# A hybrid RWKV-7 / Mamba-2 / mixture-of-experts kernel: the recurrence pairs' operands through DRAM, and the chain as a stream of its own

## The chip, the cores and the metric

The kernel runs on one core of a Trainium2 chip. The metric is the device time in microseconds (us) of one execution. The profile is that of one execution, taken by the hardware profiler. Engines: PE (TensorE, matmul), PEld (its weight loads), DVE (VectorE), ACT (ScalarE), POOL (GpSimd) and SP (SyncE, which here issues nearly all DMAs).

## What is computed

Two layers over 256 context and 256 latent tokens of width 1024, float32. What matters here is the mixing block of each layer: an RWKV-7 branch (16 heads of 64, scanned in both directions), a Mamba-2 branch (32 heads in 8 groups), two gates, and then a mixture of 32 experts. The recurrence of the RWKV-7 branch, of one head and one direction:

```python
def wkv7_scan(r, w, k, v, a, b, s0, reverse, emit):
    def step(S, inp):
        r_t, w_t, k_t, v_t, a_t, b_t = inp
        sa = jnp.einsum("bhij,bhj->bhi", S, a_t)
        S = S * w_t[:, :, None, :] + sa[..., None] * b_t[:, :, None, :] + v_t[..., None] * k_t[:, :, None, :]
        y = jnp.einsum("bhij,bhj->bhi", S, r_t) if emit else None
        return S, y
    xs = tuple(jnp.moveaxis(t, 1, 0) for t in (r, w, k, v, a, b))
    S, ys = lax.scan(step, s0, xs, reverse=reverse)
    return S, (jnp.moveaxis(ys, 0, 1) if emit else None)
```

The context tokens come first in each scan, and their final state starts the scan of the latent tokens. In the second layer only the latent tokens are put out.

## The kernel before

**Stages.** Each layer has a head (modulation, norm), the mixing stage, a merge (branch projections `psbr`, output projection `pso`), routing, and the experts. In the mixing stage three kinds of work run beside each other: 8 RWKV pairs of two heads each (`rw_prep`, `rw_solve`, `rw_chain`, `rw_out`), 8 Mamba groups (`ssm_group`) and 8 gate blocks (`gates`); layer 0 also computes the modulation of later stages there.

**A pair.** The 512 tokens are cut into 8 chunks of 64. The two heads of a pair lie in the two halves of the 128 partitions.

- `rw_prep` (L1056) projects r, k, v, and transposes v into `SU`. For each direction d, `rw_dir` (L1152) makes the decayed operands: `X` and its transpose `XT`, `Z` (the a and r rows), and with matmuls `psg` the triangular matrices `QA` (within a chunk) and `AR` (for the output).
- `rw_solve` (L1238) inverts the triangular 64x64 systems of all chunks, heads and directions at once: 31 steps on DVE, each a multiplication into `slM` and a sum into `slY`, each needing the one before. `rw_merge` completes the inverses `TT` with PE.
- `rw_chain` (L1318) turns operands by `TT` (`psat`, `psav`, `psta`, `psua`; the copies go to `at`, `av`, `QA`, `SU`), makes the chunk transitions `GT` and the output terms, and then steps the state over the chunks: 7 steps, each a matmul `psH<-St,GT` on PE and a copy `St<-psH` on DVE (direction 0) and ACT (direction 1), each needing the one before. `psY` gathers the output.
- `rw_out` (L1406) normalizes, gates, and stores the result for the merge in DRAM (`rwd`).

**The order of the work.** Nothing is issued as it is written. A `Recorder` takes all calls of a layer down, and `schedule` (L519) orders them with a list scheduler: each engine in turn gets the call that can start first by the planner's costs, ties by the latest start that still meets the due time of its stream. A stream is a label with a due time, set by `rec.at` in `mix_streams` (L1672). A call that opens a tile must find a free place: `SLOTS` says how many tiles of a name may live at once, `CLASS` how many places there are of each size. The program that results is fixed: each engine runs its own calls in that order, and waits for others by semaphores.

**What a pair holds.** `SLOTS` allows two tiles each of `SU`, `Z`, `XT`, `AR`, `QA`, `TT`, one for each direction, so one pair at a time. `rw_dir` opens them, and before the change `rw_chain` is the last to read `SU`, `Z`, `XT`, `AR` and, as a place for the turned operands, `QA`. The next pair's `rw_dir` can open its own only when that chain has read them. All four parts of a pair form one stream, with one due time:

```python
        for i in range(8):
            rec.at(1, ("rw", i), h + 60e3 + P * (i + 1))
            self.rw_prep(l, i)
            self.rw_solve(i)
            rec.tight = True
            self.rw_chain(l, i)
            rec.tight = False
            self.rw_out(l, i)
```

All recorded calls carry the line of `emit` (L682 in the profile before, L683 after the change), so the rows are told apart by tile names.

Of the kernel before, what the change touches and what calls it, by code (L numbers as in the profile page):

```python
# [21 lines left out]
NT = 512  # L22
# [52 lines left out]
def _unit_rows():  # L75

    h = (np.arange(128) // 16) % 2
    s = 2 * np.arange(16)[None, :] + h[:, None]
    return (s[:, :, None] == np.arange(32)).astype(np.float32)
# [129 lines left out]
SLOTS = {"R": 2, "sp": 2, "t5": 4, "y5": 3, "rt5": 5, "ot": 2, "z1": 4, "wst": 2, "wh": 2, "wl": 2, "rwst": 1, "rwh": 1, "rwl": 1, "r": 1,  # L209
# [3 lines left out]
CLASS = {"c4": 18, "c2": 40, "c1": 23, "ps": 8}  # L213
# [8 lines left out]
ENGINES = tuple(LAT)  # L222

# [34 lines left out]
class _Pool:  # L258
# [3 lines left out]
    def tile(self, shape, dtype, name=None, tag=None, bufs=None):  # L262
        bufs = bufs or self.bufs
        tag = tag or name
        if not self.rec.on or self.real is None:
            return self.real.tile(shape, dtype, name=name, tag=tag, bufs=bufs)
        tag = ALIAS.get(tag, tag)
        ph = self.rec.phase
        if ph == 1:
            if self.psum and tag == "g":  # L270
                tag = "t"
            if tag in SPLIT and self.rec.stream[0] in ("rw", "sh"):
# [413 lines left out]
class Kernel:  # L686
# [10 lines left out]
    def setup(self):  # L697

        self.cp = self.pool("cp")
        self.dram = self.pool("dram", space=bass.MemoryType.DRAM)  # L700
        t = lambda n, s, d=F32: self.cp.tile(s, d, name=n)
        cst = self.cst = t("cst", [128, C_WA])
        self.c = lambda o, n=128: cst[:, o:o + n]
        self.ident = cst[:, C_ID:C_ID + 128]
        self.idb = t("idb", [128, 128], BF16)
        self.unit = t("unit", [128, 512], BF16)
        self.tri = t("tri", [128, 256], F16)
        self.io = t("io", [128, 256])
        self.iota, self.low = self.io[:, 0:128], self.io[:, 128:256]
# [12 lines left out]
        self.gd = self.dram.tile([128, 16, NT], F32, name="gd")  # L722
        self.ys = self.dram.tile([N_EXP * CAP[0], D], F32, name="ys")

    def constants(self):
# [4 lines left out]
        u = t([128, 512], F32, "unit32")  # L730
        nc.sync.dma_start(u, i["unit"].rearrange("p j t -> p (j t)"))
        nc.vector.tensor_copy(self.unit, u)
        nc.sync.dma_start(self.io, i["cst"][:, C_WS:C_T64F])
# [322 lines left out]
    def rw_prep(self, l, i):  # L1056
# [23 lines left out]
        vp = rp.tile([128, 64 + NT + 64], F32, name="v", bufs=2)  # L1080
        G.memset(vp[:, 0:64], 0.0)
        G.memset(vp[:, 64 + NT:], 0.0)
        v = S["v"] = vp[:, 64:64 + NT]
# [26 lines left out]
        for w0_ in (0, 4, 8):  # L1110
            pv = self.psum("t", [128, 4, 128], "psv")
            n = min(4, 9 - w0_)
            for w in range(n):
                T.transpose(pv[:, w], vp[:, 64 * (w0_ + w):64 * (w0_ + w) + 128], self.ident)
            if w0_ < 8:
                A.activation(SU[0][64:128, w0_:w0_ + 4, 0], pv[64:128, :, 0:64], AF.Copy)
            a = 0 if w0_ else 1
            A.activation(SU[0][0:64, w0_ + a - 1:w0_ + n - 1, 1], pv[0:64, a:n, 64:128], AF.Copy)
# [118 lines left out]

    def rw_solve(self, i):  # L1238
# [16 lines left out]
        G.tensor_copy(Y.rearrange("p j t -> p (j t)"), self.unit)  # L1255
# [62 lines left out]
    def rw_chain(self, l, i):  # L1318
# [14 lines left out]
        GT = wk.tile([128, 2, 8, 64], F32, name="GT", tag="slW")  # L1333
        St = wk.tile([128, 2, 8, 64], F32, name="St", tag="X")
        PH = []

        def batch(name, cs, out, lhs, rhs):

            ps = out or self.psum("g", [128, 8, 64], name)
            with nc.together():  # L1340
                for c in cs:
                    for e in E:
                        T.matmul(ps[rows[e], c], lhs(c, e), rhs(c, e), start=True, stop=True)
            return ps

        for d in range(2):
            SU = S["SU"][d]
            TT, XT, Z, AR = [S[x, d] for x in ("TT", "XT", "Z", "AR")]
            qa = S["QA", d].rearrange("p (c e) t -> p c e t", e=2)
            all8 = range(8)  # L1350
            mid = seq[d][1:7]

            ps = batch("psat", all8, None, lambda c, e: Z[rows[e], c, 0], lambda c, e: self.ident[rows[e], 64 * e:64 * e + 64])
            at = wk.tile([128, 8, 64], F32, name="at", tag="slY")
            A.activation(at, ps, AF.Copy)
            ps = batch("psav", all8, None, lambda c, e: qa[rows[1 - e], c, e], lambda c, e: SU[rows[1 - e], c, e])
            av = wk.tile([128, 8, 64], F32, name="av", tag="slB")
            V.tensor_copy(av, ps)
# [4 lines left out]
            ps = batch("psua", all8, None, lambda c, e: TT[rows[e], c], lambda c, e: av[rows[e], c])  # L1363
            A.activation(SU[rows[0], :, 0], ps[rows[0]], AF.Copy)
            V.tensor_copy(SU[rows[1], :, 1], ps[rows[1]])
            ps = batch("psgt", mid, None, lambda c, e: qa[rows[e], c, e], lambda c, e: XT[rows[e], c, 64 * e:64 * e + 64])
# [10 lines left out]
            ps = batch("psra", range(c0, 8), None, lambda c, e: qa[rows[e], c, e], lambda c, e: AR[rows[e], 2 * c + e])  # L1377
# [28 lines left out]
    def rw_out(self, l, i):  # L1406
# [12 lines left out]
        V.scalar_tensor_tensor(gw[64:96, 1], lo[64:96, 128:256], SW, gw[64:96, 1], op0=OP.mult, op1=OP.subtract)  # L1419
        y = wk.tile([128, NT], F32, tag="ot", name="gy", bufs=3)  # L1420
# [18 lines left out]
        G.tensor_tensor(y[:, :n], y[:, :n], S["bv"][:, :n], op=OP.add)  # L1439
# [232 lines left out]
    def mix_streams(self, l):  # L1672
# [50 lines left out]
    def route(self, l, X):  # L1723
# [63 lines left out]
        V.tensor_tensor(at, E1, E2, op=OP.add)  # L1787
        pp = self.psum("g", [128, nt, 32], "pspos")
        for t in range(nt):
            for u in range(t + 1):  # L1790
                T.matmul(pp[:, t], self.low if u == t else self.c(C_ONE), at[:, u], start=u == 0, stop=u == t)
# [391 lines left out]
```

## Time and profile before

| | us |
|---|---|
| median of 3 runs (3537.98 to 3549.52) | 3539.37 |
| the profiled execution, its own time | 3538.96 |
| its span | 3537.1 |
| PE busy | 3110.2 (88%) |
| PE weight loads busy | 2094.7 (59%) |
| DVE busy | 2447.3 (69%) |
| ACT busy | 1705.4 (48%) |
| POOL busy | 769.3 (22%) |

The span is the time from the first instruction to the last. "Busy" adds the times in which an engine executes; a busy PE is not a PE at its peak, since matmuls overlap. "Granted clock" is TensorE's clock as a share of full speed. The mixing stage of layer 0 lies at about 100 to 1185 us, its experts end at about 1930 us; the mixing stage of layer 1 lies at about 2000 to 2905 us, and its experts run to the end. A row with "idle ... <- X" tells how long an engine stood before such instructions, and what ended it.

### The profile page before, as it was taken

Reading aid. Unit: us, or ns where it says so; the run is one execution under the profiler, and the core shown is the slowest. Engines: PE = TensorE matmul, PEld = TensorE weight load, DVE = VectorE, ACT = ScalarE, POOL = GpSimd, SP = SyncE. Lnnn points to the kernel's source line nnn. Section 1 sums busy time; section 2 is a strip of 40 time slices with the busy share of each in tenths; the row PEclk is TensorE's granted clock in tenths of the full one; section 3 lists DMA queues with packets and bytes.
Section 4 is the critical chain, followed back from the end, with each engine's and each line's share of the span. In section 5 each row is a group of like instructions: output and inputs, shape, how many; then the busy total and the mean of one; then the engine's idle time right before and its main releaser. Section 6 shows DMA issues by size and latency. Waiting matters only on the chain. (4 is left out here: it accounts for less than half of the span.)

```text
span 3537.1 us, 86322 instructions
## 1 busy us (share of the span) xinstructions
PE 3110.2 (88%) x36050; PEld 2094.7 (59%) x36050; DVE 2447.3 (69%) x4491; ACT 1705.4 (48%) x3155; POOL 769.3 (22%) x1080
## 2 busy tenths in 40 slices
PE   7899889898998998999998778888889789899987
PEld 3566466475566457888886455666566668333332
DVE  4868868768778337999997788788988765221112
ACT  4554454454544325998886645554545434111111
POOL 1332332333232111111111133232333311000000
PEclk9999999999999997999999899999999889899998
DMA  7032231421312736999996411221212138999996
GB/s 283 28 106 73 93 118 51 151 100 43 120 57 98 276 104 222 412 401 397 396 394 249 154 63 45 74 69 50 75 61 71 53 125 299 346 399 398 399 398 243
DMA packets 241746, 662.65 MB, mean 187 GB/s; under 512 B 26688, under 2 KB 55104, under 8 KB 241344
## 3 DMA queue, kind: packets, MB, share of 16 engines
q1 hardware_dynamic: 236608, 640.22, 49.1%
q10 hardware_dynamic: 3584, 12.58, 0.9%
q8 instruction: 287, 4.70, 0.5%
q0 software_dynamic: 1152, 4.19, 0.3%
q14 instruction: 115, 0.94, 0.1%
HBM read 622.30 MB, written 34.60 MB: 186 GB/s over the span
## 5 line engine op out<-in xcount | busy, mean ns | idle before, releaser
L682 PE MATMUL mm<-h,wh 128*128 128x512 f16 (+1 forms) x2432 | 680.4, 363 | 11.0 <-ACT wh L682 11.0
L682 PEld LDWEIGHTS <-wh 128*128 128x128 f16 x3200 | 311.4, 99 | 280.7 <-issue 25.4
L682 PE MATMUL mm<-h,wl 128*128 128x512 f16 (+2 forms) x1216 | 439.0, 362 | 39.2 <-DVE wl L682 39.1
L682 DVE SCALAR_TENSOR_TENSOR ewl<-est,ewh 128x1024 f16<-128x1024 f32 x352 | 411.7, 1222 | 15.5 <-ACT ewh L682 12.4
L682 ACT ACTIVATE ewh<-est 128x1024 f16<-128x1024 f32 x384 | 382.6, 1049 | 32.4 <-PE pse L682 28.3
L682 DVE SCALAR_TENSOR_TENSOR wl<-wst,wh 128x1024 f16<-128x1024 f32 (+1 forms) x234 | 293.2, 1267 | 35.0 <-ACT wh L682 34.5
L682 PE MATMUL pse<-xg,ewh 128*128 128x96 f16 x4096 | 276.5, 206 | 2.9 <-DVE xg L682 0.8
L682 PEld LDWEIGHTS <-ewh 128*128 128x128 f16 x4096 | 265.8, 98 | 7.1
L682 PEld LDWEIGHTS <-wl 128*128 128x128 f16 (+1 forms) x1600 | 159.4, 100 | 181.4 <-DVE wl L682 47.9
L682 PE MATMUL pse<-xg,ewl 128*128 128x96 f16 x2048 | 264.0, 206 | 0.3 <-issue 0.2
L682 ACT ACTIVATE wh<-wst 128x1024 f16<-128x1024 f32 (+1 forms) x234 | 240.2, 1043 | 12.2 <-DMA wst<-in_wmix_dram 11.6
L682 PE MATMUL pse<-esh,xg 128*64 128x512 f32 x512 | 236.3, 597 | 0.0
L682 PE MATMUL pse<-est,xg 128*64 128x512 f32 x512 | 236.3, 597 | 0.0
L682 DVE SCALAR_TENSOR_TENSOR cva<-cvz,cwh,cva 128x512 f32<-128x512 f32 (+1 forms) x256 | 204.0, 797 | 0.4
L682 PEld LDWEIGHTS <-ewl 128*128 128x128 f16 x2048 | 199.4, 98 | 5.8 <-issue 4.1
L682 DVE TENSOR_TENSOR slM<-slY,slW 128x144 f32<-128x144 f32 (+22 forms) x496 | 175.0, 353 | 6.4
L682 POOL TENSOR_TENSOR ewl<-est,ewh 128x1024 f16<-128x1024 f32 x32 | 69.7, 2180 | 487.5 <-ACT ewh L682 414.6
L682 DVE SCALAR_TENSOR_TENSOR eyl<-psy,egs,eyh 128x512 f16<-128x512 f32 x32 | 24.0, 751 | 211.2 <-ACT eyh L682 211.2
L682 PEld LDWEIGHTS <-h 128*128 128x128 f16 x2496 | 150.0, 102 | 27.0 <-issue 21.1
L682 POOL TENSOR_TENSOR sht<-shz 128x512 f32<-128x512 f32 (+3 forms) x56 | 65.2, 1164 | 403.7 <-ACT shz L682 244.4
L682 PE MATMUL psz<-wh,h 128*128 128x128 f16 x1536 | 149.4, 225 | 0.0
L682 PE MATMUL psz<-wl,h 128*128 128x128 f16 x768 | 139.9, 225 | 8.3 <-DVE wl L682 8.3
(561 smaller groups left out, 7072.7 us busy)
## 6 DMA issues: line engine op xcount, KB each, us to landing
est<-in_w_dram SPq DMA_DIRECT2D x576, 512.0 KB, 7.5
wst<-in_wmix_dram SPq DMA_DIRECT2D x246, 512.0 KB, 4.7
esh<-in_w_dram SPq DMA_DIRECT2D x384, 256.0 KB, 6.6
wst<-in_wmod_dram SPq DMA_DIRECT2D x96, 512.0 KB, 6.0
ys<-ey ACTq DMA_DIRECT2D x32, 384.0 KB, 6.9
lot<-in_lora_dram SPq DMA_DIRECT2D x16, 256.0 KB, 4.8
gd<-gat SPq DMA_DIRECT2D x16, 256.0 KB, 2.0
smd<-smo SPq DMA_DIRECT2D x16, 256.0 KB, 3.4
```

The costliest lines, as they stand in the source:

```text
L682: r = getattr(e, m)(*[real(x) for x in a], **{n: real(x) for n, x in k.items()})
```

## The change

A pair's chain no longer reads its operands where `rw_dir` left them.

- `rw_dir` now also does the two turns that need no inverse: `psat` (the a rows, copied by ACT over `Z`) and `psav` (QA times SU, copied by ACT and DVE, half each, over `SU`). Then it stores `Z`, `SU`, `XT` and `AR` of its direction in DRAM (`sd`): four DMAs from the SP queue. `bv`, which `rw_out` adds, is stored too (`sbv`).
- `rw_chain` opens `Z`, `SU`, `XT`, `AR` anew and loads them from `sd`, four DMAs a direction; `rw_out` loads `bv`. `psta` and `psua` then use `TT` as before, but the turned a rows go to `Z` in one copy on ACT; the half copy of `psta` to `QA` on DVE is gone. `QA` is last read in the solve's merge.
- Chain and output are a stream `("ch", i)` of their own, due once the next pair is prepared (`LAG = 1`).
- `GT` gets a place of its own. The shape of the transposes of v changes, so that v needs no zeroed edges (two POOL memsets fewer for a pair). The unit rows of `slY` are written as a DVE memset and a POOL copy of 32 elements, in place of a POOL copy of 512. The table `low` is loaded by the router only.

```diff
@@ _unit_rows, setup, constants: smaller tables
...
+        self.sd = self.dram.tile([128, 8, 2, 4, 1024], F32, name="sd")
+        self.sb_ = self.dram.tile([128, 8, NT], F32, name="sbv")
...
-SLOTS = {"R": 2, "sp": 2, "t5": 4, ...
+SLOTS = {"GT": 1, "t5": 4, ...
-CLASS = {"c4": 18, "c2": 40, "c1": 23, "ps": 8}
+CLASS = {"c4": 18, "c2": 41, "c1": 23, "ps": 8}
+LAG = 1
...
@@ rw_prep
         bv = S["bv"] = rp.tile([128, NT], F32, name="bv", bufs=2)
         V.tensor_tensor(bv[:, :NT - o0], pb[:, o0:], v[:, o0:], op=OP.mult)
+        nc.sync.dma_start(self.sb_[:, i, :NT - o0], bv[:, :NT - o0])
@@ rw_dir, at its end
+        rows = self.rows2
+        SU = S["SU"][d]
+        ps = self.batch("psat", lambda c, e: Z[rows[e], c, 0], lambda c, e: self.ident[rows[e], 64 * e:64 * e + 64])
+        A.activation(Z[:, :, 0], ps, AF.Copy)
+        ps = self.batch("psav", lambda c, e: QA[rows[1 - e], 2 * c + e], lambda c, e: SU[rows[1 - e], c, e])
+        A.activation(SU[rows[0], :, 0], ps[rows[0]], AF.Copy)
+        V.tensor_copy(SU[rows[1], :, 1], ps[rows[1]])
+        sd = self.sd[:, i, d]
+        nc.sync.dma_start(sd[:, 0], Z.rearrange("p c b t -> p (c b t)"))
+        nc.sync.dma_start(sd[:, 1], SU.rearrange("p c b t -> p (c b t)"))
+        nc.sync.dma_start(sd[:, 2], XT.rearrange("p c t -> p (c t)"))
+        if full:
+            nc.sync.dma_start(sd[:, 3], AR.rearrange("p c t -> p (c t)"))
+        else:
+            nc.sync.dma_start(sd[:, 3, 512:], AR[:, 8:].rearrange("p c t -> p (c t)"))
@@ rw_solve
-        G.tensor_copy(Y.rearrange("p j t -> p (j t)"), self.unit)
+        V.memset(Y, 0.0)
+        G.tensor_copy(bass.AP(tensor=Y.tensor, offset=Y.offset, ap=[Y.ap[0], [34, 16], [1, 2]]),
+                      self.unit[:, None, :].to_broadcast([128, 16, 2]))
@@ rw_chain
         for d in range(2):
-            SU = S["SU"][d]
-            TT, XT, Z, AR = [S[x, d] for x in ("TT", "XT", "Z", "AR")]
...
+            TT = S["TT", d]
+            sd = self.sd[:, i, d]
+            Z = S["Z", d] = rp.tile([128, 8, 2, 64], F32, name="Z", bufs=4)
+            nc.sync.dma_start(Z.rearrange("p c b t -> p (c b t)"), sd[:, 0])
+            SU = rp.tile([128, 8, 2, 64], F32, name="SU", bufs=4)
+            nc.sync.dma_start(SU.rearrange("p c b t -> p (c b t)"), sd[:, 1])
+            XT = rp.tile([128, 8, 128], F32, name="XT", bufs=4)
+            nc.sync.dma_start(XT.rearrange("p c t -> p (c t)"), sd[:, 2])
+            AR = rp.tile([128, 16, 64], F32, name="AR", bufs=4)
+            nc.sync.dma_start(AR[:, 2 * c0:].rearrange("p c t -> p (c t)"), sd[:, 3, 128 * c0:])
...
-            ps = batch("psta", all8, None, lambda c, e: TT[rows[e], c], lambda c, e: at[rows[e], c])
-            A.activation(qa[rows[0], :, 0], ps[rows[0]], AF.Copy)
-            V.tensor_copy(qa[rows[1], :, 1], ps[rows[1]])
+            ps = batch("psta", lambda c, e: TT[rows[e], c], lambda c, e: Z[rows[e], c, 0])
+            A.activation(Z[:, :, 0], ps, AF.Copy)
@@ mix_streams
             self.rw_prep(l, i)
             self.rw_solve(i)
+            rec.at(1, ("ch", i), h + 60e3 + P * (i + 1 + LAG) + 1e3)
             rec.tight = True
             self.rw_chain(l, i)
```

The change moves instructions on every engine, since the scheduler sees other tiles and due times. Two places of the order show it.

DVE, layer 1, the steps of the chain of pair 2 (`St<-psH`), before; `slM` and `slY` are the solve, `smo` and `yg` the Mamba group, `wl` a weight's low half:

```order
L682 COPY SU<-psua 64x8x64
L682 TENSOR_SCALAR yg<-yg,yrr 128x256
L682 TENSOR_SCALAR St<-psH,pl 128x64
L682 TENSOR_TENSOR GT<-psgt,id_65 128x192 x2
L682 TENSOR_TENSOR Z<-Z,psra 128x4x64 x2
L682 TENSOR_SCALAR St<-psH,pl 128x64 x5
L682 CAST smo<-yt 128x256
L682 TENSOR_TENSOR smo<-yt,smo 128x256
L682 TENSOR_SCALAR St<-psH,pl 128x64
L682 SCALAR_TENSOR_TENSOR wl<-wst,wh 128x1024
L682 CAST smo<-yt 128x256
L682 TENSOR_TENSOR smo<-yt,smo 128x256
```

The same place after the change:

```order
L683 TENSOR_TENSOR Z<-Z,psra 128x4x64
L683 TENSOR_SCALAR St<-psH,pl 128x64
L683 TENSOR_TENSOR slM<-slY,slW 128x144
L683 TENSOR_SCALAR cva<-cvz,cwh,cbh 128x512
L683 TENSOR_REDUCE slY<-slM 128x8
L683 SCALAR_TENSOR_TENSOR cva<-cvz,cwh,cva 128x512
L683 TENSOR_SCALAR St<-psH,pl 128x64
L683 TENSOR_TENSOR slM<-slY,slW 128x152
L683 SCALAR_TENSOR_TENSOR wl<-wst,wh 128x1024
L683 TENSOR_SCALAR St<-psH,pl 128x64
L683 TENSOR_REDUCE slY<-slM 128x8
L683 SCALAR_TENSOR_TENSOR cva<-cvz,cwh,cva 128x512
```

Between one step of the chain and the next there now stand two instructions of the next pair's solve and one of a Mamba convolution or a weight, where five steps stood one behind the other.

The SP queue, layer 1, around the preparation of pair 4, before; `wst` are weights, `smd`, `gd`, `rwd` results for the merge, `w0t`, `log`, `lot` small tables:

```order
L682 DMA w0t<-in_w_dram 128x2x128
L682 DMA rwd<-rwq 128x2x256
L682 DMA wst<-in_wmix_dram 128x1024
L682 DMA log<-in_lora_dram 128x256
L682 DMA wst<-in_wmix_dram 128x1024
L682 DMA lot<-in_lora_dram 128x512
L682 DMA wst<-in_wmix_dram 128x1024 x7
L682 DMA smd<-smo 128x2x256 x2
L682 DMA gd<-gat 128x256
```

The same place after the change (`sd` in DRAM holds the operands):

```order
L683 DMA sbv<-bv 128x256
L683 DMA bv<-sbv 128x256
L683 DMA wst<-in_wmix_dram 128x1024
L683 DMA sd<-XT 128x1024
L683 DMA XT<-sd 128x1024
L683 DMA sd<-AR 128x512
L683 DMA AR<-sd 128x512
L683 DMA sd<-Z 128x1024
L683 DMA Z<-sd 128x1024
L683 DMA sd<-SU 128x1024
L683 DMA SU<-sd 128x1024
```

The stores of pair 4's operands and the loads of pair 3's now alternate tile by tile, since a load needs the place that the store before it frees. Eight more such DMAs follow these rows, with one weight load among them.

## Rows read from the trace of the kernel before

**Rows 1.** The two mixing stages by engine: busy us (count), TensorE clock, DMA share, GB/s.

```profile
100.00:1185.00 1085.00, 972.82 (x11812) 657.03 (x11811) 826.29 (x1688) 518.58 (x1159) 337.00 (x485) 0.96 0.28 97
2000.00:2905.00 905.00, 757.28 (x9421) 558.05 (x9420) 745.49 (x1567) 448.73 (x972) 287.98 (x471) 0.92 0.20 63
```

**Rows 2.** The same view in stretches of 100 us.

```profile
300.00:400.00 100.00, 95.36 (x1361) 68.96 (x1360) 76.13 (x147) 54.50 (x130) 36.20 (x50) 1.00 0.32 104
1500.00:1600.00 100.00, 98.60 (x1700) 83.57 (x1698) 97.65 (x105) 91.35 (x115) 13.76 (x6) 1.00 1.02 402
2500.00:2600.00 100.00, 86.31 (x1130) 63.08 (x1127) 85.90 (x186) 52.74 (x116) 35.36 (x57) 0.95 0.21 64
2800.00:2900.00 100.00, 75.43 (x1012) 58.92 (x1012) 78.89 (x176) 37.65 (x80) 22.31 (x37) 0.83 0.28 89
```

**Rows 3.** Waits of DVE, layer 0's mixing: idle us in total, times, longest us.

```profile
DVE St L682 <- PE psH L682: 30.6, 39, 1.3
...
DVE Z L682 <- PE psra L682: 13.0, 16, 1.4
...
DVE SU L682 <- PE psua L682: 8.3, 12, 1.5
...
DVE GT L682 <- PE psgt L682: 6.0, 9, 1.6
```

**Rows 4.** Waits of DVE, layer 1's mixing.

```profile
DVE St L682 <- PE psH L682: 23.7, 34, 1.0
...
DVE Z L682 <- PE psra L682: 7.5, 8, 1.3
...
DVE SU L682 <- PE psua L682: 4.4, 10, 1.6
...
DVE GT L682 <- PE psgt L682: 3.6, 7, 0.6
```

**Rows 5.** Timeline of DVE in one chain: start, length, last the idle time before it.

```profile
2349.18 0.89 DVE L682 TENSOR_TENSOR Z<-Z,psra 128x256 f32<-128x256 f32 x2 [0.51 <-PE psra L682]
...
2351.22 0.28 DVE L682 TENSOR_SCALAR St<-psH,pl 128x64 f32<-128x64 f32 x1 [0.96 <-PE psH L682]
2352.36 0.28 DVE L682 TENSOR_SCALAR St<-psH,pl 128x64 f32<-128x64 f32 x1 [0.86 <-PE psH L682]
2353.50 0.28 DVE L682 TENSOR_SCALAR St<-psH,pl 128x64 f32<-128x64 f32 x1 [0.86 <-PE psH L682]
```

**Rows 6.** Groups of DVE by line and shape: count | busy us, mean ns | idle us before.

```profile
L682 DVE COPY QA<-psta 64x512 f32<-64x512 f32 x32 | 22.2, 695 | 6.2 <-ACT QA L682 2.7 <-PE psta L682 2.5
```

**Rows 7.** The same view of ACT.

```profile
L682 ACT ACTIVATE wh<-wst 128x1024 f16<-128x1024 f32 x230 | 238.4, 1052 | 12.2 <-DMA wst<-in_wmix_dram 11.6
...
L682 ACT ACTIVATE at<-psat 128x512 f32<-128x512 f32 x32 | 19.1, 597 | 3.9 <-PE psat L682 3.6
...
L682 ACT ACTIVATE QA<-psta 64x512 f32<-64x512 f32 x32 | 18.9, 590 | 27.3 <-DVE QA L682 23.4 <-PE psta L682 3.8
...
L682 ACT ACT_TABLE_LOAD x7 | 9.0, 1283 | 0.9 <-PEq L2173 0.7
```

**Rows 8.** The same view of POOL.

```profile
L682 POOL CAST slY<-unit 128x512 f32<-128x512 bf16 x16 | 12.2, 765 | 0.1
...
L682 POOL MEMSET v<- 128x64 f32 x32 | 3.8, 155 | 0.3
```

**Rows 9.** Tile Z on DVE: duration ns min/median/max.

```profile
L682 DVE SCALAR_TENSOR_TENSOR Z<-kkt,P x32: 679/948/1661, 116.3 to 2810.2; 128x512 f32<-128x512 f32 x32
```

**Rows 10.** DMA issues: count, KB each, median us from issue to landing.

```profile
wst<-in_wmix_dram SPq DMA_DIRECT2D x246, 512.0 KB, 4.7
...
xd<-xres SPq DMA_DIRECT2D x6, 512.0 KB, 3.0
```

**Rows 11.** Tile wst on SP: issue ns min/median/max.

```profile
L682 SPq DMA_DIRECT2D wst<-in_wmix_dram x250: 327/328/1287, 26.5 to 2967.5; - x125
```

**Rows 12.** Waits of the SP queue, layer 1's mixing.

```profile
SPq L682 <- DVE wl L682: 325.5, 22, 49.8
```

More of the change, by code (lines that the diff above doesn't have):

```diff
@@ L271, in tile @@
                 tag = "t"
-            if tag in SPLIT and self.rec.stream[0] in ("rw", "sh"):
+            if tag in SPLIT and self.rec.stream[0] in ("rw", "sh", "ch"):
                 tag = "r" + tag
@@ L729, in constants @@
         nc.vector.tensor_tensor(self.id2, self.ident[:, 0:64], self.ident[:, 64:128], op=OP.add)
[L730 to L733, printed above, removed]
+        nc.sync.dma_start(self.unit, i["unit"])
+        nc.sync.dma_start(self.iota, i["cst"][:, C_IOTA:C_IOTA + 128])
         u = t([128, 256], F32, "tri32")
@@ L1079, in rw_prep @@
         k = S["k"] = rp.tile([128, NT], F32, name="k", bufs=2)
[L1080 to L1083, printed above, removed]
+        v = S["v"] = rp.tile([128, NT], F32, name="v", bufs=2)
         ps = self.psum("mm", [128, NT])
@@ L1109, in rw_prep @@
         S["SU"] = SU
-        for w0_ in (0, 4, 8):
+        for w0_ in (0, 4):
             pv = self.psum("t", [128, 4, 128], "psv")
[L1112 to L1116, printed above, removed]
+            with nc.together():
+                for w in range(4):
+                    if w + w0_:
+                        T.transpose(pv[:, w], v[:, 64 * (w0_ + w) - 64:64 * (w0_ + w) + 64], self.ident)
+            if not w0_:
+                with nc.together():
+                    T.matmul(pv[64:128, 0], v[:, 0:64], self.ident, start=True, stop=True)
+                    T.matmul(pv[0:64, 0], v[:, NT - 64:NT], self.ident, start=True, stop=True)
+                A.activation(SU[0][0:64, 7, 1], pv[0:64, 0, 64:128], AF.Copy)
+            A.activation(SU[0][64:128, w0_:w0_ + 4, 0], pv[64:128, :, 0:64], AF.Copy)
             a = 0 if w0_ else 1
-            A.activation(SU[0][0:64, w0_ + a - 1:w0_ + n - 1, 1], pv[0:64, a:n, 64:128], AF.Copy)
+            A.activation(SU[0][0:64, w0_ + a - 1:w0_ + 3, 1], pv[0:64, a:4, 64:128], AF.Copy)
         G.tensor_copy(SU[1][64:128, :, 0], SU[0][64:128, :, 0])
@@ L1236, in rw_dir, with batch @@
                                     mi[:, None, :].to_broadcast([128, 4, 64]), op=OP.mult)
+        rows = self.rows2
[13 more added lines that the diff above has]
+            nc.sync.dma_start(sd[:, 3, 512:], AR[:, 8:].rearrange("p c t -> p (c t)"))
+    rows2 = (slice(0, 64), slice(64, 128))
+    def batch(self, name, lhs, rhs, cs=range(8)):
+        ps = self.psum("g", [128, 8, 64], name)
+        with self.nc.together():
+            for c in cs:
+                for e in range(2):
+                    self.nc.tensor.matmul(ps[self.rows2[e], c], lhs(c, e), rhs(c, e), start=True, stop=True)
+        return ps
     def rw_solve(self, i):
@@ L1332, in rw_chain @@
         yo = lambda c, e: py[rows[e], 64 * c - o0:64 * c - o0 + 64]
-        GT = wk.tile([128, 2, 8, 64], F32, name="GT", tag="slW")
+        GT = wk.tile([128, 2, 8, 64], F32, name="GT")
         St = wk.tile([128, 2, 8, 64], F32, name="St", tag="X")
         PH = []
[L1337 to L1344, printed above, removed]
@@ L1346, in rw_chain @@
-        for d in range(2):
-            SU = S["SU"][d]
-            TT, XT, Z, AR = [S[x, d] for x in ("TT", "XT", "Z", "AR")]
-            qa = S["QA", d].rearrange("p (c e) t -> p c e t", e=2)
-            all8 = range(8)
-            mid = seq[d][1:7]
[L1353 to L1358, printed above, removed]
-            ps = batch("psta", all8, None, lambda c, e: TT[rows[e], c], lambda c, e: at[rows[e], c])
-            A.activation(qa[rows[0], :, 0], ps[rows[0]], AF.Copy)
-            V.tensor_copy(qa[rows[1], :, 1], ps[rows[1]])
-            ps = batch("psua", all8, None, lambda c, e: TT[rows[e], c], lambda c, e: av[rows[e], c])
+        batch = self.batch
@@ L1376, in rw_chain @@
                                  skip_group_check=True)
-            ps = batch("psra", range(c0, 8), None, lambda c, e: qa[rows[e], c, e], lambda c, e: AR[rows[e], 2 * c + e])
+            ps = batch("psra", lambda c, e: Z[rows[e], c, 0], lambda c, e: AR[rows[e], 2 * c + e], range(c0, 8))
             V.tensor_tensor(Z[:, c0:, 1], Z[:, c0:, 1], ps[:, c0:], op=OP.add)
@@ L1790, in route @@
             for u in range(t + 1):
-                T.matmul(pp[:, t], self.low if u == t else self.c(C_ONE), at[:, u], start=u == 0, stop=u == t)
+                T.matmul(pp[:, t], low if u == t else self.c(C_ONE), at[:, u], start=u == 0, stop=u == t)
         pos = tl("pos")
```

19 lines of the change are left out of this document (11 added, 8 removed).

## The prediction

> **What bounds the kernel now.** I read the two mixing stages by engine first, since the change touches nothing else. Layer 0's lasts 1085 us and PE is busy in 972.8 of them (89.7%), DVE in 826.3 (76.2%); layer 1's lasts 905 us, PE 757.3 (83.7%), DVE 745.5 (82.4%) [rows 1]. No engine is full over a whole stage, and DMA works at 0.28 and 0.20. The stretches then tell what a stage can reach: PE is 95.4% busy in layer 0's best stretch, while a middle one of layer 1 has PE at 86.3% and DVE at 85.9%, and the last one of layer 1 falls to 75.4% and 78.9% at a granted clock of 0.83 [rows 2]. So layer 0 is near PE's limit, and layer 1 is held by the order in which work becomes ready, with DVE the nearest engine to a limit.
>
> Third, the waits of DVE: in layer 0 it stands 30.6 us before steps of the chain (St<-psH), and 13.0, 8.3 and 6.0 before the chain's other copies, 57.9 in all [rows 3]; in layer 1 it is 23.7 + 7.5 + 4.4 + 3.6 = 39.2 [rows 4]. Together 97.1 us. The timeline of one chain shows how it comes about: a step of 0.28 us every 1.14 us, and 0.86 us of nothing between [rows 5]. DVE has no other work there, because the next pair cannot be prepared until this chain has read its operands. The solve, DVE's longest string of work in a pair, and the chain thus never lie beside each other.
>
> **What goes away.** With the operands in DRAM the places come free when preparation ends, so the next pair's solve lies beside the chain; the order after the change shows two solve instructions and one other between steps. How much of the idle time is filled is the main unknown, and I bound it by shares.
>
> Work on DVE first. One of two half copies of `psta` goes: 32 x 695 ns = 22.2 us [rows 6]. The copy of `psav` was one whole DVE copy and is now half ACT, half DVE; I take that as no change on DVE, since a half has the same 512 elements for a partition. The memset of `slY` is added, 16 times; the nearest row is a memset on another engine, 155 ns [rows 8], so 2.5 us. Net -19.7 us, 9.85 a layer. POOL's copy of the unit rows shrinks (16 x 765 ns = 12.2 us [rows 8] at most), and two memsets for a pair go: POOL is busy 31% of these stages [rows 1], so nothing.
>
> Layer 1, by DVE: 745.5 - 9.9 = 735.6 us of work. At today's share of 82.4% that is 893 us (-12); at the share of the middle stretch, 85.9% [rows 2], it is 856 (-49). I take the middle, **-30**: a stage has a start and a tail that no overlap fills, but the tail is where two pairs' work now shares what one pair's did.
>
> Layer 0, by PE, whose work stays: 972.8 us. At today's 89.7% nothing is won; at the best stretch's 95.4% the stage lasts 1020 (-65). Middle **-32**. Sum -62, ends -12 and -114. As a cross-check: -62 means 19.7 us of work saved and 42 of the 97.1 us of chain idle used, somewhat under half. That suits a layer 0 where PE is nearly full and a freed DVE helps only now and then.
>
> **What it adds.** *DMAs.* 145 more for a layer, all on SP, 290 x 0.33 us = 96 us of issue [rows 11], beside a queue that in layer 1 alone stands 325.5 us waiting for weight places to come free [rows 12]. Bytes: sixteen transfers of 512 KB for a pair plus `bv`, nearly 9 MB in layer 0 and 7.6 in layer 1, where half of `AR` isn't moved; 132 MB in all. The experts' stretch moves 402 GB/s [rows 2], at which rate it is 22 and 19 us for a pair, 328 us altogether if nothing hid it. But the pairs are 1085/8 = 136 and 905/8 = 113 us apart, so the DMA share would rise by 0.16 and 0.17, to 0.44 and 0.37: hidden. *The order on SP* is the weaker cover. A load needs the place of a store that was issued just before it, and a store of 512 KB lands 3.0 us after its issue [rows 10]; eight such couples for a pair are 24 us in which SP can issue no weight. A weight load is due every (1085 + 905)/246 = 8 us and takes 4.7 to land [rows 10]. Those behind the couples come late. What stands behind a late weight: ACT's cut of its high half `wh`, then DVE's `wl`, then the projections on PE. Today ACT waits 11.6 us in all for such loads [rows 7]; I allow as much again on the path, **+12**; below, 0, if the couples fall where SP would have waited for places anyway; above, the slower rival.
>
> *ACT.* The whole `psat` and `psta` copies cost about 0.6 us as the halves do [rows 7]; 32 half copies more for `psav` are about 32 x 590 ns = 19 us, on an engine at 48 to 50% [rows 1]: hidden, and ACT loses a wait of 23.4 us for DVE before its half of `psta` [rows 7]. If ACT were the limit at these places, this would cost 19. Two more table loads of 1283 ns [rows 7] stand in layer 0's head, before the mixing: I take them as hidden behind its loads, else 2.6.
>
> *Contention.* One operation with the same shape, Z<-kkt,P on DVE, takes from 679 to 1661 ns [rows 9], and POOL is busy 31% of the time. If every one of the 42 us that DVE gains met a POOL of 31% and stood still for it, that would give back 13; I take 0, since POOL's own work shrinks. The Trainium skill (SBUF — State Buffer, Who interferes with whom) says that a DVE instruction with two SBUF inputs contends with a GpSimd instruction that reads SBUF, and the solve's multiplications would be such instructions; by it the sum would be up to 13 us less good, 3502. The spread of the Z row agrees with it but doesn't prove it.
>
> **The sum.** -62 + 12 = -50 against the profiled execution's 3538.96 us, which stands 0.4 us under the median: **3489 us**. Ends of the forecast itself: with the costs of 19 and 13 paid it is -50 + 32 = -18, 3521; with no lateness and two thirds of the way to the best shares it is -80, 3459.
>
> **Rivals.** *Only the work counts.* PE sets both stages, and the idle time on DVE was free. Then only the 19.7 us saved remain, 3519. For it: PE at 95.4% in layer 0. Against: layer 1's PE at 83.7%.
>
> *DVE is the bound of both stages.* Then all the 97.1 us are used and 19.7 saved, -117: 3422. For it: weight loads of PE are busy in only 61 and 62% of the stages [rows 1], so PE's rows may hold slack; against, layer 0's PE stretches. The Trainium skill (Perfetto Trace Analysis, Identifying the Most-Contended Engine) says that matmul busy time is a bad measure of headroom and that the busy share of weight loads should be read instead; by that rule this rival would be the forecast, 3422. No row here shows which measure holds; the stages' lengths after the change will.
>
> *SP's queue becomes the bound (slower).* If the couples come in one block, 24 us without weights exceed the 8 us by which the next is due, and PE stands 16 us. Were that so in half of the 16 pairs, 128 - 62 = +66: 3605. It decides when ACT's waits for weight loads pass about 60 us, five times today's. For it: the block of eight couples in the order with only one weight load in it. Against: SP stands 325 us in layer 1 waiting for places, which means that weights are mostly loaded ahead of their use.
>
> *The chain becomes the late one.* A step on DVE now stands behind two or three instructions of about 1 us, so a chain of 7 steps lasts twice as long, and PE may wait for St where it waited for nothing; where the chain ends a stage, this takes back the gain: about 3539.
>
> **Chances.** Forecast 0.62, only the work 0.15, DVE the bound 0.08, SP the bound 0.09, late chain 0.06. The range takes in the forecast's ends, only-the-work and the late chain, with a margin below for a fill between mine and the deep one: 3450 to 3541. That leaves out 0.08 and 0.09 and little of the forecast. A change under 0.3% (10.6 us) cannot be told from none here. The first three cases are all faster by more than that, 0.85, of which 0.02 lie at the upper edge of the only-the-work case; so faster 0.83, same 0.08 (late chain and that edge), slower 0.09.
>
> **What would show it.** DVE's idle before St<-psH, 54.3 us today, under 15. Layer 1's DVE share at 84.5% or more, and both stages shorter by some 25 us. ACT's wait for weight loads under 24 us. PE's waits for St under 20 us in all. If the idle before St is gone and the stages are as long as before, PE was the bound and the fill was worth nothing; if ACT's wait for weights is over 60, the queue was; if PE waits for St, the chain was. A DVE Z<-kkt,P median well above 948 ns would point to contention.

## The result, and the profile after

The changed kernel takes 3481.69 us (median of 4 runs, 3478.62 to 3486.49) against 3541.14 us of the kernel before in the same runs: ratio 0.983, 95% interval 0.9808 to 0.9851, so 53 to 68 us faster. The forecast was 3489 in a range of 3450 to 3541.

The profile below is of an execution of 3483.44 us. First the span and the first part of its page, the busy time of each engine:

```profile
span 3480.9 us, 86869 instructions
...
PE 3122.1 (90%) x36082; PEld 2099.9 (60%) x36082; DVE 2422.3 (70%) x4474; ACT 1722.0 (49%) x3189; POOL 773.5 (22%) x1048
```

DVE's work fell by 25.0 us against the page before (2447.3), PE's rose by 11.9. The two mixing stages by engine, with the columns of [rows 1]; layer 0's now ends 11 us earlier, and layer 1's, which starts 9 us earlier, is 41 us shorter:

```profile
100.00:1174.00 1074.00, 987.26 (x11814) 663.80 (x11813) 827.16 (x1674) 521.89 (x1169) 337.39 (x470) 0.95 0.46 163
1991.00:2855.00 864.00, 759.75 (x9474) 559.66 (x9473) 718.01 (x1560) 456.49 (x986) 284.28 (x457) 0.94 0.41 140
```

Beside [rows 1]: in layer 0 DVE has the same work as before (826.3, now 827.2) and 12 us less idle time; in layer 1 it has 27.5 us less work (745.5, now 718.0) and 13.5 less idle time. These add up to the 52 us of both stages. DMA's share rose from 0.28 to 0.46 and from 0.20 to 0.41; the prediction had 0.44 and 0.37.

What DVE waits for in layer 0's mixing, with the columns of [rows 3]:

```profile
DVE wl L683 <- ACT wh L683: 33.7, 25, 4.6
...
DVE smo L683 <- ACT yt L683: 19.1, 10, 3.3
...
DVE St L683 <- PE psH L683: 10.4, 6, 5.8
...
DVE GT L683 <- PE psgt L683: 3.0, 4, 1.9
...
DVE SU L683 <- PE psua L683: 1.1, 2, 0.6
DVE Z L683 <- PE psra L683: 0.9, 2, 0.6
```

and in layer 1's, to be held against [rows 4]:

```profile
DVE zt L683 <- ACT zt L683: 13.0, 5, 5.3
DVE lw L683 <- PE psw L683: 11.1, 8, 2.5
...
DVE GT L683 <- PE psgt L683: 3.4, 1, 3.4
...
DVE St L683 <- PE psH L683: 1.8, 3, 0.8
...
DVE SU L683 <- PE psua L683: 1.1, 1, 1.1
```

The four waits of the chain are down from 57.9 to 15.4 us in layer 0 and from 39.2 to 6.3 in layer 1, by 75.4 us. Before `SU<-psua`, however, only the name of what ends the wait has changed: DVE now waits there for ACT, which copies the other half (count | busy us, mean ns | idle us before, of the whole span, before and after):

```profile
L682 DVE COPY SU<-psua 64x512 f32<-64x512 f32 x32 | 22.2, 695 | 13.0 <-PE psua L682 12.7
...
L683 DVE COPY SU<-psua 64x512 f32<-64x512 f32 x32 | 22.2, 694 | 14.0 <-ACT SU L683 9.2 <-PE psua L683 2.2 <-issue 1.9
```

So some 64 us of idle time in the chain are gone (42.1 before `St`, 19.6 before `Z`, 3.2 before `GT`, none before `SU`). But DVE's idle time as a whole is only 25.4 us less. The other 39 came back in front of other work: `wl<-ACT wh` rose from 15.3 to 33.7 and `smo` from 7.9 to 19.1 in layer 0, `zt` from 2.1 to 13.0 and `lw` from 2.4 to 11.1 in layer 1 (the four earlier numbers are of the same view of the kernel before). Most of it is waiting for ACT: added up over this view, DVE's waits for ACT rose from 72.9 to 110.1 us in layer 0 and from 31.3 to 42.0 in layer 1. ACT for its part has a new wait, for the turned a rows of the chain:

```profile
ACT Z L683 <- PE psta L683: 75.9, 28, 7.2
```

That this wait holds up ACT's other work, and so DVE, is not shown: in e3, below, it is 33.2 us with the same time of the kernel.

The timeline of DVE in layer 1's third chain shows the overlap, in the place of [rows 5]:

```profile
2355.89 0.28 DVE L683 TENSOR_SCALAR St<-psH,pl 128x64 f32<-128x64 f32 x1
2356.08 0.30 DVE L683 TENSOR_TENSOR slM<-slY,slW 128x144 f32<-128x144 f32 x1
2356.30 0.55 DVE L683 TENSOR_SCALAR cva<-cvz,cwh,cbh 128x512 f32<-128x512 f32 x1
2356.76 0.30 DVE L683 TENSOR_REDUCE slY<-slM 128x8 f32<-128x144 f32 x1
2356.97 0.74 DVE L683 SCALAR_TENSOR_TENSOR cva<-cvz,cwh,cva 128x512 f32<-128x512 f32 x1
2357.63 0.28 DVE L683 TENSOR_SCALAR St<-psH,pl 128x64 f32<-128x64 f32 x1
```

Between two steps of the chain (`St<-psH`) stand solve instructions of the next pair (`slM`, `slY`) and a convolution or a weight, and no idle time. A step now comes 1.7 us after the one before it (1.3 to 1.7 in this chain) and not 1.14: the chain is slower, and DVE is full while it runs.

PE has new waits too, for the chain's operands; PE over the whole span, the operands from DRAM (`sd`) and the state:

```profile
PE psta L683 <- DMA Z<-sd: 13.1, 13, 2.6
...
PE psua L683 <- DMA SU<-sd: 10.2, 9, 2.3
...
PE psH L683 <- DVE St L683: 2.5, 5, 0.6
...
PE psY L683 <- DMA AR<-sd: 2.1, 2, 1.5
...
PE psY L683 <- DVE St L683: 0.8, 1, 0.8
```

25.4 us of waits for loads, and 3.3 for the state. SP, in contrast, hardly stands for the stores; all its waits of that kind:

```profile
SPq L683 <- DMA sd<-AR: 4.2, 2, 2.9
...
SPq L683 <- DMA sd<-SU: 3.3, 2, 1.7
...
SPq L683 <- DMA sd<-Z: 2.6, 2, 2.1
...
SPq L683 <- DMA sd<-XT: 1.2, 1, 1.2
```

### The profile page after: what moved, and what is told of

Read it like the earlier page. It is cut to its first block, busy times and chain, and to the rows that moved or that the text cites. A ratio compares the mean times of both kernels' runs of the same rounds, so it can differ in the third digit from the quotient of the medians.

```text
span 3480.9 us, 86869 instructions
## 1 busy us (share of the span) xinstructions
PE 3122.1 (90%) x36082; PEld 2099.9 (60%) x36082; DVE 2422.3 (70%) x4474; ACT 1722.0 (49%) x3189; POOL 773.5 (22%) x1048
## 5 line engine op out<-in xcount | busy, mean ns | idle before, releaser
L683 ACT ACTIVATE wh<-wst 128x1024 f16<-128x1024 f32 (+1 forms) x234 | 238.8, 1039 | 12.1 <-DMA wst<-in_wmix_dram 11.7
L683 DVE TENSOR_TENSOR slM<-slY,slW 128x144 f32<-128x144 f32 (+22 forms) x496 | 168.0, 339 | 8.3
L683 ACT ACTIVATE eu<-pse 128x384 f32<-128x384 f32 (+1 forms) x64 | 34.4, 538 | 243.3 <-PE pse L683 243.3
L683 DVE TENSOR_REDUCE slY<-slM 128x2 f32<-128x4 f32 (+23 forms) x496 | 147.1, 297 | 6.4
```

What stands on the lines that cost most here:

```text
L683: r = getattr(e, m)(*[real(x) for x in a], **{n: real(x) for n, x in k.items()})
```

## The experiments

The layers are compared by three instants of each profile: the first `psbr<-rwt` on PE (layer 0's mixing is over), the last `pse<-xg,ewh` (layer 0's experts are over) and the last store `rwd<-rwq` (layer 1's mixing is over). "Layer 0" is the first instant, "layer 1" the third less the second. The median and the ratio are from all timed runs, each ratio to the kernel before on the same chip (its median was 3541 to 3544 us there). The last two columns are from one profiled execution each, and executions of one kernel differ: those of e1 lay between 3530.85 and 3550.03.

| run | median us | ratio to before, interval | layer 0 | layer 1 |
|---|---|---|---|---|
| before | 3541.14 | 1 | 1185.4 | 985.9 |
| the change | 3481.69 | 0.9830 (0.9808 to 0.9851) | 1173.6 | 944.4 |
| e1 trip, one stream | 3540.47 | 0.9997 (0.9985 to 1.0010) | 1212.1 | 978.9 |
| e2 edits, no trip | 3509.53 | 0.9915 (0.9900 to 0.9930) | 1182.8 | 965.9 |
| e3 stores on ACT | 3480.06 | 0.9835 (0.9819 to 0.9850) | 1154.6 | 943.8 |
| e4 stores twice | 3482.38 | 0.9847 (0.9828 to 0.9866) | 1171.4 | 943.2 |
| e5 DVE + solve's head | 3547.17 | 1.0010 (0.9998 to 1.0023) | 1205.5 | 978.5 |
| e6 the same, before | 3614.78 | 1.0204 (1.0184 to 1.0224) | 1219.3 | 1026.4 |
| e7 PE + | 3499.08 | 0.9871 (0.9850 to 0.9893) | 1159.2 | 967.3 |
| e8 the same, before | 3547.30 | 1.0005 (0.9994 to 1.0015) | 1185.6 | 992.9 |
| e9 DVE + in the gates | 3511.71 | 0.9912 (0.9888 to 0.9936) | 1179.0 | 965.4 |
| e10 the same, before | 3584.05 | 1.0116 (1.0092 to 1.0139) | 1189.6 | 1023.6 |
| e11 halves on ACT | 3472.82 | 0.9801 (0.9779 to 0.9823) | 1141.4 | 963.8 |
| e12 the same, layer 0 alone | 3460.87 | 0.9773 (0.9753 to 0.9794) | 1138.4 | 946.1 |

**e1: the trip, without a stream of its own.**

```diff
-            rec.at(1, ("ch", i), h + 60e3 + P * (i + 1 + LAG) + 1e3)
```

> The operands go through DRAM, but the chain stays in the stream of its pair, with its pair's due time; in the order no step of a chain then has a solve instruction behind it on DVE. Theory A (the gain is the next pair's solve filling the chain's idle time on DVE): the overlap is gone and the trip is paid, 3535 to 3560 us, with DVE's idle before St<-psH back at about 50 us. Theory B (the gain is the work saved by the reshaped operands, and the tiles that come free early): 3480 to 3500 us.

Measured: the time of the kernel before. DVE's idle time in the chain, in layer 0's mixing, is back:

```profile
DVE St L683 <- PE psH L683: 36.8, 35, 2.4
```

and so it is in layer 1 (24.6 us).

**e2: the edits, without the trip.** The stores are left out, and the chain and the output read what the preparation left; one stream for a pair:

```diff
-            sd = self.sd[:, i, d]
-            Z = S["Z", d] = rp.tile([128, 8, 2, 64], F32, name="Z", bufs=4)
...
+            Z, SU, XT, AR = S["Z", d], S["SU"][d], S["XT", d], S["AR", d]
...
-        GT = wk.tile([128, 2, 8, 64], F32, name="GT")
+        GT = wk.tile([128, 2, 8, 64], F32, name="GT", tag="slW")
```

> Only the edits of the operands (psat and psav ahead of the solve, psta in one ACT copy, the transposes of v, slY by a memset): no trip through DRAM, one stream for a pair. Theory A: what DVE saves and no more, 3520 to 3535 us. Theory B: nearly all of the gain, 3480 to 3500 us. The difference of this run and the one with the trip in one stream is the price of the trip: 0 to 10 us if it is hidden, 20 to 30 if SP's queue is held by it.

Measured: 3509.53, between the two theories. The two mixing stages of e2, with the columns of [rows 1], from 100 and from 1997 us on:

```profile
100.00:1183.00 1083.00, 982.19 (x11843) 669.64 (x11840) 825.60 (x1680) 525.00 (x1178) 344.34 (x472) 0.95 0.28 98
1997.00:2883.00 886.00, 762.46 (x9467) 559.26 (x9465) 728.83 (x1561) 456.26 (x989) 288.85 (x461) 0.93 0.21 67
```

DVE has 16.7 us less work than before in layer 1 and layer 1 is 20.0 shorter; in layer 0 both hardly move. The three ratios split the result: the edits are worth 1 - 0.9915, or 30 us; the trip on top of them costs 0.9997 / 0.9915, or 29 us; the stream of its own gives 0.983 / 0.9997, or 59 us (each known to some 5 to 9 us by its intervals). By the profiles the last is 38.5 us in layer 0 and 34.5 in layer 1; e1's execution was the slowest of its kernel, so these are rather high. Theory A holds for the largest part, but the edits do more than the work that I counted. Of their 30 us, the two stages of e2's profile show 23; some 7 more lie behind layer 1's mixing (621.4 us in place of 628.3), where the kernel before with added work, e6, e8 and e10, took 621.9 to 628.2, so that these 7 may be scatter. And the 29 us are the price of the trip in one stream only: no run has the overlapped chain without the trip, and so none gives its price there.

**e3: the operand stores on ACT's queue**, `nc.scalar.dma_start` in place of `nc.sync.dma_start` at the five stores of `sd`.

> The changed kernel, with its operand stores issued from ACT's queue in place of SP's, so that a store on SP no longer stands between weight loads. If the trip holds SP's queue on the path (the +12 us that the prediction allowed): 3462 to 3474 us. If the trip is hidden: 3478 to 3490 us, ACT being at half load. If issuing on ACT costs there more than on SP: above 3490.

**e4: the stores twice**, the second time to another place in DRAM (of `AR` the half that both layers have):

```diff
+        se = self.se[:, i, d]
+        nc.sync.dma_start(se[:, 0], Z.rearrange("p c b t -> p (c b t)"))
+        nc.sync.dma_start(se[:, 1], SU.rearrange("p c b t -> p (c b t)"))
+        nc.sync.dma_start(se[:, 2], XT.rearrange("p c t -> p (c t)"))
+        nc.sync.dma_start(se[:, 3, 512:], AR[:, 8:].rearrange("p c t -> p (c t)"))
```

> The changed kernel, with each operand tile stored a second time into another place in DRAM: 128 more stores on SP, some 58 MB. If the trip is hidden: within 6 us of the changed kernel, 3476 to 3488 us. If its transfers or SP's queue lie on the path: 0.33 us of issue each is 42 us, and each load waits for one more store, 3500 to 3530 us.

Measured: neither can be told from the changed kernel (0.9835 and 0.9847 beside 0.983). So beside the overlapped chain neither the stores' bytes nor their standing on SP's queue are on the path; the loads were not probed in this way. How far SP's standing matters is shown by the waits of e3, where loads wait for stores that another queue issued:

```profile
SPq L683 <- DMA sd<-AR: 89.0, 16, 10.8
SPq L683 <- DMA sd<-XT: 75.2, 12, 10.9
...
SPq L683 <- DMA sd<-SU: 62.9, 14, 10.7
...
SPq L683 <- DMA sd<-Z: 16.4, 6, 5.1
```

243.5 us of standing, against 11.3 in the changed kernel, with the same time of the kernel. In e1, too, SP stood long for stores, 158.5 us, but the traces do not make this the explanation of the 29 us: ACT's waits for weight loads are 14.5 us in e1 and 15.0 in e2. What the trip costs in one stream stays open. From solve to solve layer 0 takes 138.1 us in e1 and 133.2 in e2. e1's mixing stages have 25 us more of PE busy time than e2's at a lower granted clock (0.94 and 0.91 against 0.95 and 0.93), but also another order of the Mamba and gate work, and no run here separates order from transfer.

**e5 to e8: what bounds a stage.** Work was added that changes no result, though the planner orders each kernel anew: ten memsets a pair in front of the solve (e5, and e6 in the kernel before), or the transposes of v made three times (e7, e8).

```diff
-        V.memset(Y, 0.0)
+        for _ in range(11):
+            V.memset(Y, 0.0)
```

```diff
-                for w in range(4):
+                for w in 3 * list(range(4)):
```

> The changed kernel with ten more memsets of slY on DVE for each pair: 160 x 485 ns = 78 us of work on DVE, 39 a layer. If DVE alone sets both stages: +78, about 3560 us. If PE sets both and DVE has slack (the rival in which only the work counts): +0 to 15, 3482 to 3497. If PE sets layer 0 and DVE layer 1, as the prediction has it: +25 to 50, 3507 to 3532, nearly all of it in layer 1.

> The kernel before with the same 160 memsets on DVE, 78 us. If DVE's idle time in the chain was time on the path, work put ahead of the solve lengthens both stages nearly by its own length: +50 to 78, 3590 to 3620 us. If PE sets the stages: +0 to 20, 3541 to 3561.

> The changed kernel with the transposes of v made three times over: 14 more on PE for a pair, 224 x 279 ns = 62 us, 31 a layer. If PE sets both stages: +62, about 3544 us. If DVE does: +0 to 15, 3482 to 3497. If PE sets layer 0 alone: +30 to 45, 3512 to 3527, nearly all of it in layer 0.

> The kernel before with its transposes of v made three times over: 18 more on PE for a pair, 288 x 278 ns = 80 us, 40 a layer. If PE sets both stages: +80, about 3621 us. If PE sets layer 0 alone: about +40, 3581. If the order of the work and DVE set both: +0 to 25, 3541 to 3566.

Measured: DVE's 78 us cost 64 in the changed kernel (1.0010 - 0.9830) and 72 in the kernel before. The transposes cost 15 and nothing that can be told from none. Their expectation was mis-sized: I had multiplied the count by the mean duration of one, but matmuls overlap, and their group's busy time rose by less. The group of the kernel before (count | busy us, mean ns), where 144 of 279 ns are 23.2 us:

```profile
L682 PE MATMUL psv<-cst,v 128*128 128x128 f32 x144 | 23.2, 279 | 0.8 <-DVE v L682 0.8
```

and in e8:

```profile
L682 PE MATMUL psv<-cst,v 128*128 128x128 f32 x432 | 57.1, 275 | 0.8 <-DVE v L682 0.8
```

So e8 added 33.9 us of PE time, some 17 in each layer, and e7, counted in the same way, 24.0. In the kernel before, the 17 us moved layer 0 by 0.2 and layer 1 by 7.0, and the whole by nothing that can be told from none (1.0005). In the changed kernel layer 0 became 14 us shorter by added work and layer 1 23 longer with 12 added: there another order weighs more than the work, and e7 decides nothing by layer.

**e9, e10: the same memsets off the pair's path**, five on the tile `gat` of each of the 16 gate blocks of a layer, ahead of its use:

```diff
             t = self.wk.tile([128, NT], F32, name="gat", bufs=1)
+            for _ in range(5):
+                nc.vector.memset(t, 0.0)
```

> The changed kernel with the same 160 memsets of 485 ns on DVE (78 us), but in the gate blocks, on a tile that no pair reads, in place of the head of the solve. If DVE's time as such sets the stages: about as much as at the solve's head, +50 to 65, 3532 to 3547 us. If the string of one pair's preparation and solve sets them, and the memsets only lengthened that string: +0 to 20, 3482 to 3502.

> The kernel before with the same memsets in the gate blocks. If DVE's time sets the stages: +50 to 70, 3591 to 3611 us. If the string of a pair does: +0 to 25, 3541 to 3566, since the idle time in the chain can then take the memsets.

The added group of e9, by line and shape (count | busy us, mean ns | idle us before):

```profile
L683 DVE MEMSET gat<- 128x512 f32 x160 | 77.6, 485 | 18.7 <-DVE gat L683 13.9 <-issue 0.3 <-DVE gw L683 0.2
```

Measured: 29 us in the changed kernel, 41 in the one before, both between the theories; the layers explain it. Of the 39 us added to a layer, layer 0 takes 4 in the kernel before and 5 in the changed one, layer 1 takes 38 and 21. At the head of the solve the same work cost 34 and 40 before, 32 and 34 after. So in the kernel before **layer 0 was set by the string of one pair after the other** (work on that string counts, work beside it hardly does), and **layer 1 by DVE** (work counts wherever it stands); by e8, PE set neither. In the changed kernel layer 0 is set as before, while in layer 1 the 21 beside the string and the 34 on it leave open how much is DVE's time and how much the string. Each of these numbers compares two executions, so 4, 5 or 7 us are not told from none.

**e11, e12: less on DVE.** The second halves of `psav` and `psua` go to ACT, in e12 in layer 0 alone.

```diff
-        V.tensor_copy(SU[rows[1], :, 1], ps[rows[1]])
+        A.activation(SU[rows[1], :, 1], ps[rows[1]], AF.Copy)
```

> The changed kernel with both halves of psav and of psua copied by ACT: 64 x 694 ns = 44 us less on DVE, 64 half copies more on ACT (49% busy). If DVE sets the stages, at 0.8 us for each us of its work as the memsets at the solve's head gave: -20 to -36, 3446 to 3462 us. If the longer string ACT, then ACT, ahead of psgt and the chain eats it: within 8 us of the changed kernel, 3474 to 3490.

> As the run before with the halves of psav and psua on ACT, but in layer 0 alone; layer 1 keeps the order of the changed kernel. In that run layer 0's mixing ended 32 us earlier than in the changed kernel and layer 1 took 19 longer. If the two layers add up independently: -32, about 3450 us. If layer 0's gain was that of one execution, or layer 1's loss follows from layer 0: 3465 to 3480.

Measured: e11 is 9 us faster than the changed kernel by the medians, with intervals that overlap. By layer it gained 32 us in layer 0 and lost 19 in layer 1. There 22.2 us of copies were gone from DVE, but its busy time was 718.3 us against 718.0 (the columns of [rows 1], from 1960 us on):

```profile
1960.00:2843.00 883.00, 766.06 (x9452) 568.30 (x9451) 718.29 (x1526) 476.30 (x1018) 296.88 (x457) 0.91 0.39 135
```

Three groups that the edit left alone ran longer by nearly as much: `X<-b,Pi` by 10.9 us, `Z<-kkt,P` by 5.6 and `wl` by 5.1. So DVE won nothing there. Why they ran longer, and what the 19 us are, is open; e7 had such scatter of an order too. e12 takes the one without the other: 3460.87 us, 0.9773 of before, an interval wholly under that of the changed kernel, and the fastest version here. About 3450 was expected if the layers add up independently, and its profiled execution took 3450.1; but the median lies 11 higher, so that they add up only in part.

## Why the prediction was right, and where its parts were not

**The sum was right by errors that cancel, which is luck.** I had 32 us less in layer 0, 30 less in layer 1, and 12 more for lateness on SP. In the two profiles layer 0 gave 12 and layer 1 gave 41, and no run shows the lateness: one term was 20 too large, one 11 too small, and one of 12 stood for a cost that isn't seen. The ratios split the result in another way, into 30 for the edits and 59 for the stream less 29 for the trip, where I had 62 less 12; but these 29 were measured in one stream, and e3 and e4 find no such cost beside the overlapped chain.

**Layer 0, "by PE, whose work stays": this step failed.** I read 89.7% as nearly full and asked how near to 95.4% the share could come. e8 shows that this share was no limit: 17 us more of PE's work left layer 0 as long as it was. The limit was the string of the pairs, as e6 and e10 show: one pair's preparation, solve and chain before the next. The starts of the solves, by the transposes that open it, in layer 0 and layer 1 of the kernel before (duration, first and last start):

```profile
L682 DVE STREAM_TRANSPOSE slW<-slB x8: 1924/1955/1974, 141.4 to 1074.5; 128x1024 f32<-128x1024 f32 x8
...
L682 DVE STREAM_TRANSPOSE slW<-slB x8: 1892/1936/1977, 2067.7 to 2821.5; 128x1024 f32<-128x1024 f32 x8
```

and of the changed one:

```profile
L683 DVE STREAM_TRANSPOSE slW<-slB x8: 1894/1954/1958, 152.4 to 1062.3; 128x1024 f32<-128x1024 f32 x8
...
L683 DVE STREAM_TRANSPOSE slW<-slB x8: 1922/1954/1960, 2054.4 to 2759.2; 128x1024 f32<-128x1024 f32 x8
```

Over 7 periods that is 133.3 us from solve to solve in layer 0 before and 130.0 after, in layer 1 107.7 and 100.7. So the chain left the string, since its steps now lie beside a solve, but the string got shorter by little: in layer 0 23 us over the stage, of which 11 went again because the first solve starts at 152.4 and not 141.4. That is why layer 0 gave 12 us in these two profiles where I had 32.

The DVE timeline tells where the little came from, and it is not from the place that the chain left. From its transposes to its last sum `slY<-slM`, a solve of layer 0 took 52.4 us before and 47.9 after (means of the first seven), and from there to the next solve it was 80.9 us before and 82.1 after; in layer 1 51.4 and 44.3, then 56.3 and 56.4. Before, the last step of a chain came 24 to 29 us after the end of its solve; these are not missing from the 80.9 and 56.3. What took their place in layer 0 is a later start of the next pair's preparation. The last sum of a solve there and an early product of the next pair's preparation, before (where the next solve starts at 672.0) and after (at 658.5):

```profile
558.39 0.75 DVE L682 SCALAR_TENSOR_TENSOR k<-shz,mu,sht 128x512 f32<-128x512 f32 x1
...
596.00 0.40 DVE L682 TENSOR_REDUCE slY<-slM 128x8 f32<-128x248 f32 x1
...
567.87 0.41 DVE L683 TENSOR_REDUCE slY<-slM 128x8 f32<-128x248 f32 x1
...
609.92 0.75 DVE L683 SCALAR_TENSOR_TENSOR k<-shz,mu,sht 128x512 f32<-128x512 f32 x1 [1.68 <-ACT sht L683]
```

Before, this product stood 77 to 114 us ahead of the next solve, mostly beside the solve before it; after, 44 to 75 us ahead, when that solve has ended or is about to. The prediction's premise that the next pair could not be prepared before the chain has read its operands holds for `rw_dir` only. Why the planner starts a pair later now is not shown.

The rule of the Trainium skill that I had set against my choice (Perfetto Trace Analysis, Identifying the Most-Contended Engine: matmul busy time is a bad measure of headroom) was borne out by e8 (33.9 us more of PE's work at a ratio of 1.0005). The result that I had drawn from it, 3422, was not: PE had room, but of DVE's 97 us of idle time in the chain some 64 are gone, and 39 came back as other waits. A full use of it would also have needed the string to shrink by as much.

**Layer 1, "by DVE": the step held, its size was low.** e10 shows DVE as the bound of the kernel before, at 38 us for 39. I had 30 us less; measured were 41. Of this, 27.5 is less work on DVE, where I had counted 9.85. The part that I had mis-sized downwards was the memset of `slY`, 485 ns and not the 155 of POOL's row (which had 64 elements for a partition, where this has 512), 7.8 us in both layers instead of 2.5; the half copy of `psav` costs what the whole one did (688 ns), as taken:

```profile
L683 DVE COPY SU<-psav 64x512 f32<-64x512 f32 x32 | 22.2, 694 | 8.8 <-ACT SU L683 4.5 <-PE psav L683 3.4
```

What made up for it was no removed instruction: the rest of DVE's work in layer 1 ran shorter, `X<-b,Pi` 854 ns in place of 1106, and `gw` 285 in place of 921 (groups of the same shape in layer 1 of the two traces):

```profile
L682 DVE TENSOR_TENSOR X<-b,Pi 64x512 f32<-64x512 f32 x32 | 35.4, 1106 | 0.8 <-ACT Pi L682 0.4
...
L683 DVE TENSOR_TENSOR X<-b,Pi 64x512 f32<-64x512 f32 x32 | 27.3, 854 | 0.9
```

In layer 0 it went the other way: DVE's work there rose by 0.9 us where I had counted 9.85 less, with `X<-b,Pi` at 1126 ns in place of 973. The copies gone and the memsets added are 7 us less a layer; the rest of both differences, some 20 us less in layer 1 and 8 more in layer 0, is the lengths of instructions that no edit touched, a term that I had put at 0. The row that I had named as its sign:

```profile
L683 DVE SCALAR_TENSOR_TENSOR Z<-kkt,P x32: 676/693/1672, 123.7 to 2752.7; 128x512 f32<-128x512 f32 x32
```

has a median of 693 ns where it was 948 [rows 9], but that overstates the change: the mean fell from 1039 to 991 only, from 949 to 838 in layer 1 and not at all in layer 0 (1130, now 1145). I had put up to 13 us on this by the Trainium skill's rule on two SBUF inputs (SBUF — State Buffer, Who interferes with whom). The row shows no such loss, and no run tested whether meeting POOL is what makes these lengths.

**The lateness on SP, +12: the term had the wrong mechanism.** I had SP stand 24 us for each pair between a store and the load behind it. It stands 11.3 us in all, because a load does not need the place of the store ahead of it, as I had read the order:

```profile
2331.66 0.32 SPq L683 DMA_DIRECT2D sd<-XT  x1
2332.03 0.42 SPq L683 DMA_DIRECT2D XT<-sd  x1
```

The load is issued 0.37 us after the store, and no transfer of `XT` landed in under 2.6 us; three quarters of the loads follow the store of their name within 1.5 us. The planner counts two tiles of a name, so in its order the load comes after the store that ends a tile, but it gives the load whichever place of that size came free first. ACT's wait for weight loads is as short as it was, 11.7 us against 11.6 [rows 7], as the forecast asked (under 24):

```profile
L683 ACT ACTIVATE wh<-wst 128x1024 f16<-128x1024 f32 x230 | 237.0, 1048 | 12.0 <-DMA wst<-in_wmix_dram 11.7
```

The cost of the trip that the trace shows is another one: PE waits 25.4 us for operands that were loaded late. In e3 these waits are gone and the time is the same, so they too are not shown to be on the path.

**The other signs.** Idle before St<-psH is 10.4 + 1.8 = 12.2 us, foretold under 15. PE's waits for St are 3.3 us, under 20: the late chain never came. Layer 1's DVE share is 83.1% where I asked for 84.5%: its work fell by 27.5 us while the stage got 41 shorter. The stages were to be some 25 us shorter each; they are 11 and 41. Of the rivals, "only the work counts" comes near the edits alone (30 us measured, 20 expected), though not by its reason, PE; and the slower one, the queue as bound, fell with e3 and e4.

## What to carry to other kernels

A busy share says little about what added or removed work will cost. A probe does: add a known amount of work to one engine, once on the suspected string and once beside it, and read each stage; here 39 us cost 34 on the string and 4 beside it in one layer, and 40 and 38 in the next. Moving operands through DRAM paid here only as the means to give the chain a stream of its own: the same trip without that gave nothing. After a step is taken out of a string, measure the string again: here the stretch that the chain left kept its length. And idle time that a change fills is won only as far as no other wait takes its place: of some 64 us filled here, 25 stayed.

## What the runs showed of the hardware

- An in-order DMA queue can stand for long at no cost: SP stood 243.5 us for stores in e3, 11.3 in the changed kernel, with the same time. Twice the stores (58.7 MB more) cost nothing measurable either; the median weight load then landed 6.5 us after its issue, in the changed kernel 6.1, in the kernel before 4.7.
- A memset of 128x512 f32 on DVE takes 485 ns, which is 70% of a copy of 64x512 f32 out of PSUM (694), which has as many elements for a partition.
- Instructions that no edit touched changed their mean duration between two orders by up to a factor of 3 (`gw<-log,gw` 921 and 285 ns in layer 1; `X<-b,Pi` 1106, 854 and in e11 1194), enough to make or undo some 20 us of DVE's time in a stage. What makes them longer was not tested.
